# A transformer step in Strassen blocks: sums of weight blocks moved from GpSimd to VectorE

## The chip, the cores and the metric

The kernel runs on one core of a Trainium2 chip. The core has a matrix engine (TensorE, in the profile PE, with its weight loads as PEld), and VectorE (DVE), ScalarE (ACT), GpSimd (POOL) and SyncE (SP), each with a queue that it works off in order; they wait for one another through semaphores. The metric is the time of the slowest core in device microseconds, the median of several executions.

## The reference

One inference step of a one-layer hybrid encoder over 640 tokens (512 of a prompt, 8 times 16 of samples) at a width of 2048, all in float32:

```python
a = rms_norm(x, g_mix); proj = a @ w_in            # q, k, v, forget logits, u
attn = fox_attend(...)                             # 8 heads of 128
ssm = s5_mixer(u, ...)                             # 64 groups, complex diagonal state, GLU
merged = concat(rms_norm(attn), rms_norm(ssm))
h = x + merged @ w_out                             # 2048 x 2048
f = rms_norm(h, g_ffn)
h = h + (silu(f @ w_gate) * (f @ w_up)) @ w_down   # 2048 x 5632, twice, and back
gate = sigmoid(rms_norm(h, g_ple) @ w_ple_gate)    # 2048 x 2048
h = h + gate * (p_i @ w_ple_proj)
```

It returns h with keys, values, log forget values and states.

## The kernel before, in words

Up to about 770 us of the span the kernel computes the input projections, the attention and the state-space part; the change touches little there. Behind that come five matrix products, all made in the same way: the output projection (name o, 8 products), gate and up (g and u, 22 each, in turn), down (d, 28 cells) and the gate of the layer's input embedding (p, 8, called the last projection here).

Each of these products is a 2x2 block product by Strassen's scheme in Winograd's form: seven block products in place of eight. One product works over weight blocks, called units in the code: 328 in all, each 128x1024 float32 (four quarters of 256 columns), four per product in o, g, u and p, and two to four per cell in down. From the four quarters come four sums (`ws`), so that seven stationary operands exist. To keep float32 accuracy each operand is cut in two: a rounded copy (`wh`, ScalarE, line 86) and the remainder (`wl`, VectorE, line 87), in two pieces, first the three raw quarters (768 columns), then the four sums (1024 columns). A unit takes 42 matmuls of 320 columns: seven products, two halves of the rows, and three pairs of high and low parts (lines 1205 to 1207). The staged block `wst` has two buffers, `wh` and `wl` two each, and the sums `ws` one. Of the four sums of a unit GpSimd makes three (lines 109 to 111) and VectorE one (line 112).

The moving side, the activations, is cut in the same way: four quarters (128x320 each) and three sums, made by `winograd_rows` (four operations, lines 118 to 121; one of them overwrites a quarter), then a rounded copy and a remainder (`cut`, lines 1050 and 1051). Results that a later stage reads as activations are summed on GpSimd and stored in DRAM (`keep`); a later `fetch` loads and cuts them. The tiles are called `km` for o (built by `build`), `kf` for gate and up, `kt` for down, `kh` for the last projection.

After the seven block products of a cell the banks of PSUM are evicted (lines 1231 to 1240): two copies on ScalarE, six additions on VectorE, and one addition on GpSimd (line 1240). The first copy, line 1232, marks each eviction in the trace. Then o adds x, d adds the stored h (`accum_op` in a DMA from GpSimd's queue for cells that are not the last of their row, line 1346), and p multiplies and adds the stored h on GpSimd (line 1373).

The program is written in this order, and a planner with modelled costs lays out each engine's queue: in the trace, sums of the next unit stand between the additions of an eviction.

Of the kernel before, what the change touches and what calls it, by code (L numbers as in the profile page):

```python
# [9 lines left out]
F32 = mybir.dt.float32  # L10
# [4 lines left out]
OP = mybir.AluOpType  # L15
# [89 lines left out]

def winograd_weights(nc, q, s):

    tt = nc.gpsimd.tensor_tensor
    tt(s[:, 0], q[:, 0], q[:, 3], op=OP.add)  # L109
    tt(s[:, 1], s[:, 0], q[:, 1], op=OP.subtract)  # L110
    tt(s[:, 3], q[:, 2], s[:, 1], op=OP.subtract)  # L111
    nc.vector.tensor_tensor(s[:, 2], q[:, 1], q[:, 0], op=OP.subtract)


def winograd_rows(eng, q, s):

    tt = eng.tensor_tensor
    tt(s[:, 0], q[:, 0], q[:, 1], op=OP.subtract)  # L118
    tt(q[:, 0], q[:, 2], q[:, 0], op=OP.subtract)
    tt(s[:, 1], q[:, 2], s[:, 0], op=OP.subtract)  # L120
    tt(s[:, 2], s[:, 1], q[:, 3], op=OP.subtract)  # L121
# [43 lines left out]
def hybrid_step(ctx: ExitStack, tc: tile.TileContext, io):  # L165
    nc = tc.nc
# [32 lines left out]
    tc_dr = dp.tile([FT // 2, P, 7, NH2], F32, name="tc_dr")  # L199
    fc_dr = dp.tile([KT // 2, P, 7, NH2], F32, name="fc_dr")  # L200
    hc_dr = dp.tile([KT // 2, P, 7, NH2], F32, name="hc_dr")
# [819 lines left out]
    for k in range(8):  # L1021
        t = gp_.tile([P, NTOK], F32, tag="xg", name=f"gld{k}", bufs=3)
# [4 lines left out]
    for k in range(2):  # L1027
        t = gp_.tile([P, NTOK], F32, tag="xg", name=f"p{k}", bufs=3)
# [17 lines left out]
    def rows(dram, j):  # L1046
        return dram[2 * j * P : 2 * (j + 1) * P, :].rearrange("(a p) n -> p a n", p=P)

    def cut(k, part, x, eng=nc.vector):
        nc.scalar.activation(k[:, 0, part], x, AF.Copy)  # L1050
        eng.tensor_tensor(k[:, 1, part], x, k[:, 0, part].bitcast(F32), op=OP.subtract)  # L1051

    def blocks4(x):
        return x.rearrange("p a (h n) -> p (a h) n", h=2)

    def build(k, b, s, src, i, by):

        nc.sync.dma_start(b, rows(src, i))
        nc.vector.tensor_tensor(b, b, by[:, None, :].to_broadcast([P, 2, NTOK]), op=OP.mult)
        q = blocks4(b)  # L1060
        cut(k, slice(1, 4), q[:, 1:])
        winograd_rows(nc.gpsimd, q, s)
        cut(k, slice(0, 1), q[:, 0:1])
        cut(k, slice(4, 7), s)
        return k
# [6 lines left out]
    def build_early(i):  # L1072
        b = gp_.tile([P, 4, 512], F32, tag="kc", name=f"mb{i}", bufs=2)
        s = gp_.tile([P, 2, 8, P], F32, tag="vc", name=f"ms{i}", bufs=1)
        b = b.rearrange("p a n -> p (a n)")[:, : 2 * NTOK].rearrange("p (a n) -> p a n", a=2)
        s = s.rearrange("p a b n -> p (a b n)")[:, : 3 * NH2].rearrange("p (a n) -> p a n", a=3)
        mk.append(build(kp_view(act_tile(f"km{i}")), b, s, m_dr, i, ssqa if i < 4 else ssqs))
# [65 lines left out]
    def pair(name):  # L1143
        return fo.tile([P, 2, NTOK], F32, tag="R", name=name, bufs=2)
# [12 lines left out]
    def kp_tile(name, i):  # L1157
        if i < 5:
            return kp_view(act_tile(name))
        if i == 5:  # L1160
            return fo.tile([P, 2, 7, NH2], F32R, tag="kp", name=name, bufs=1)
        return xp.tile([P, 2, 7, NH2], F32R, tag="kp", name=name, bufs=KB)

    def seven(name):
        return xp.tile([P, 7, NH2], F32, tag="c7", name=name, bufs=1)

    def keep(eng, c, dram, i):

        winograd_rows(eng, c[:, :4], c[:, 4:])
        nc.sync.dma_start(dram[i], c)  # L1170

    def whole(k, x, eng=nc.vector):
        cut(k, slice(0, 4), x[:, :4])
        cut(k, slice(4, 7), x[:, 4:], eng)
        return k

    later = {}

    def fetch(name, slot, dram, i, eng=nc.vector, late=False):
        k = kp_tile("k" + name, slot)  # L1180
        x = k[:, 1].bitcast(F32)
        nc.sync.dma_start(x, dram[i])
        if late:
            later.setdefault(i // 2 - 2, []).append(lambda: whole(k, x, eng))
            return k
        return whole(k, x, eng)

    def cut_late(u):
        for f in later.pop(u, ()):
# [36 lines left out]
    def strassen(name, kps, after=None, into=None):  # L1226
        ps = products(name, kps, after)
        r = pair("r" + name) if into is None else into
        r11, r12, r21, r22 = blocks(r)
        q = fo.tile([P, NH2], F32, tag="q", name="q" + name, bufs=1)  # L1230
        tt = nc.vector.tensor_tensor
        nc.scalar.activation(q, ps[1], AF.Copy)
        tt(r11, q, ps[2], op=OP.add)
        nc.scalar.activation(r12, ps[3], AF.Copy)
        tt(q, q, ps[6], op=OP.add)
        tt(r22, q, ps[7], op=OP.add)
        tt(r12, r12, ps[5], op=OP.add)
        tt(r21, r22, ps[4], op=OP.subtract)
        tt(r22, r22, ps[5], op=OP.add)
        nc.gpsimd.tensor_tensor(r12, r12, q, op=OP.add)  # L1240
        return r
# [6 lines left out]
    def squares(s, x, t, first, other=nc.vector):  # L1248
        nc.scalar.activation(t, x, AF.Square)
        if first:  # L1250
            nc.vector.tensor_tensor(s, t[:, 0], t[:, 1], op=OP.add)
        else:
            nc.vector.tensor_tensor(s, s, t[:, 0], op=OP.add)
            other.tensor_tensor(s, s, t[:, 1], op=OP.add)
# [4 lines left out]
    for i in range(5, 8):  # L1259
        s = seven(f"sm{i}")  # L1260
# [3 lines left out]
    def scaled(c, x, gain, j):  # L1264

        for a in range(2):
            nc.scalar.activation(c[:, 2 * a : 2 * a + 2], halves(x[:, a]), AF.Copy, scale=gain[:, 2 * j + a : 2 * j + a + 1])

    fk = []
    for j in range(8):  # L1270
        after = None
        if j == 7:
            def after(u):
                for i in (2 * u, 2 * u + 1):
                    if i < 7:
                        fk.append(fetch(f"f{i}", i, fc_dr, i, nc.gpsimd if i == 3 else nc.vector, i == 6))
        r = strassen(f"o{j}", mk, after)
        x = pair(f"x{j}")
        nc.sync.dma_start(x, io["xT"][2 * j : 2 * j + 2].rearrange("a p n -> p a n"))
        nc.vector.tensor_tensor(r, r, x, op=OP.add)  # L1280
        c = seven(f"c{j}")
        scaled(c, r, gffn, j)
        if j < 7:
            keep(nc.gpsimd, c, fc_dr, j)
        else:
            winograd_rows(nc.gpsimd, c[:, :4], c[:, 4:])
            kf7 = kp_tile("kf7", 7)
            fk.append(kf7)
            later.setdefault(1, []).append(lambda: whole(kf7, c))
        nc.sync.dma_start(rows(h_dr, j), r)  # L1290
        squares(ssqh, r, x, j == 0)

    tk, slots = {}, (0, 1, 2, 3, 4, 5, 6, 7)

    def next_t():

        u = len(tk) // 2
        if u < FT // 4:
            for i in (2 * u, 2 * u + 1):
                tk[i] = fetch(f"t{i}", slots[i % 8], tc_dr, i, nc.gpsimd if i == 3 else nc.vector)  # L1300

    for f in range(FT // 2):
        z = strassen(f"g{f}", fk, cut_late if f == 0 else None)
# [9 lines left out]
        c = seven(f"t{f}")  # L1313
        t = c[:, :4].rearrange("p (a h) n -> p a (h n)", a=2)
# [13 lines left out]
    def next_h():  # L1328
        i = ready.pop(0)
        hk[i] = fetch(f"h{i}", hslot[i], hc_dr, i)  # L1330

    for n, (j, us, first, last) in enumerate(cells):
        def after(i, us=us, n=n):
            uses[us[i]] -= 1
            if not uses[us[i]] and n < len(cells) - 4:
                next_t()
            if n < 2 and i:
                next_t()
            if n == len(cells) - 1:
                for _ in range(min(2, 3 - i)):  # L1340
                    if ready:
                        next_h()

        r = strassen(f"d{n}", [tk[i] for u in us for i in (2 * u, 2 * u + 1)], after)
        if not last:
            nc.gpsimd.dma_start(rows(h_dr, j), r, accum_op=OP.add)
            continue
        x = pair(f"hx{j}")
        nc.sync.dma_start(x, rows(h_dr, j))
        nc.vector.tensor_tensor(r, r, x, op=OP.add)  # L1350
        c = seven(f"hc{j}")
        scaled(c, r, gple, j)
        if j in (3, 4, 5):
            winograd_rows(nc.gpsimd, c[:, :4], c[:, 4:])
            hk[j] = whole(kp_tile(f"kh{j}", hslot[j]), c)
        else:
            keep(nc.gpsimd, c, hc_dr, j)
            ready.append(j)
        nc.sync.dma_start(rows(h2_dr, j), r)
        squares(ssqp, r, x, j == 4)  # L1360
    hk = [hk[i] for i in (4, 5, 6, 7, 0, 1, 2, 3)]
    for j in range(7):
# [5 lines left out]
        x = pair(f"pj{j}")  # L1368
        nc.sync.dma_start(x, rows(pj_dr, j))
        nc.vector.tensor_tensor(z, z, x, op=OP.mult)  # L1370
        x = pair(f"hy{j}")
# [5 lines left out]
    x = pair("pj7")  # L1377
# [6 lines left out]
    q = fo.tile([P, NH2], F32, tag="q", name="qp7", bufs=1)  # L1384
    tt = nc.vector.tensor_tensor
# [141 lines left out]
```

## Time and profile before

| | |
|---|---|
| median of 3 runs | 3037.12 us (3029.13 to 3037.15) |
| the profiled execution | 3029.73 us, its span 3027.9 us |
| TensorE, weight loads | 2850.7 us (94%), 2719.3 us (90%) |
| VectorE | 2042.4 us (67%), 2830 instructions |
| GpSimd | 1540.3 us (51%), 1545 instructions |
| ScalarE | 1237.7 us (41%), 1627 instructions |
| mean granted clock of TensorE | 0.983 of full speed |

The span is that of the instructions on the core; the time of the execution is a little longer. Busy time is the union of an engine's instructions. Durations of neighbouring instructions of one engine overlap by some hundredths of a microsecond, and a duration holds what the instruction waits for once it has begun.

### The profile page before, as it was taken

To read this page: it belongs to the slowest core of one execution; us is meant where nothing else is said; L and a number is where in the kernel's file an instruction comes from. 1 tells how busy PE (TensorE), PEld (TensorE's weight loads), DVE (VectorE), ACT (ScalarE), POOL (GpSimd) and SP (SyncE) were. 2 spreads that over 40 slices of the span, in tenths; PEclk is the share of its full clock that TensorE was granted. 3 is DMA by queue.
4 is the path that set the end of the run, shared out by engine and by line. 5 is a ranking of instruction groups with operands and counts; after the bars stand their busy time and mean duration, and the time that the engine had idled before them with its cause. 6 is when DMAs were issued, how large, how long until landed. Compare 5 with 4: busy or idle time off the path is not lost.

```text
span 3027.9 us, 48370 instructions
## 1 busy us (share of the span) xinstructions
PE 2850.7 (94%) x19051; PEld 2719.3 (90%) x19051; DVE 2042.4 (67%) x2830; ACT 1237.7 (41%) x1627; POOL 1540.3 (51%) x1545
## 2 busy tenths in 40 slices
PE   7899999999789889999999999999989999988898
PEld 6789988888788889999999999999989999987887
DVE  8939254455777786666666666666775667788766
ACT  4333365456633443333333333333434344444432
POOL 5612300000666665656565656565564554666665
PEclk9999999999899999999999999999999999999999
DMA  5565744456444623232323232323555455646443
GB/s 165 155 172 168 227 173 154 173 200 209 169 150 159 244 85 117 98 118 98 117 99 115 99 115 99 114 99 114 213 127 164 110 171 164 168 155 243 135 146 129
DMA packets 137494, 449.24 MB, mean 148 GB/s; under 512 B 14097, under 2 KB 34673, under 8 KB 124465
## 3 DMA queue, kind: packets, MB, share of 16 engines
q1 hardware_dynamic: 120032, 396.47, 38.6%
q0 software_dynamic: 15936, 45.47, 6.0%
q10 hardware_dynamic: 1296, 4.20, 0.4%
q8 instruction: 149, 2.44, 0.3%
q14 instruction: 81, 0.66, 0.1%
HBM read 342.25 MB, written 101.18 MB: 146 GB/s over the span
## 4 chain that ended last, share of the span: by engine, by line
POOL 23%; DVE 15%; PE 12%; issue 8%; ACT 6%; DMA 1%; DVEq 0%; POOLq 0%; SPq 0%; ACTq 0%
POOL ws L110 7%; DVE wl L87 7%; POOL ws L109 6%; ACT wh L86 5%; POOL ws L111 5%; PE d L1207 4%; PE d L1205 4%; PE d L1206 4%; POOL t L121 1%; POOL t L118 1%; DVE t L1257 1%; DVE rg L1257 1%; POOL rp L1373 1%; DVE kt L1051 1%; POOL t L120 1%
## 5 line engine op out<-in xcount | busy, mean ns | idle before, releaser
L86 ACT ACTIVATE wh<-ws 128x1024 fp32r<-128x1024 f32 x328 | 347.2, 1058 | 976.4 <-POOL ws L111 957.9
L87 DVE TENSOR_TENSOR wl<-ws,wh 128x1024 fp32r<-128x1024 f32 x328 | 415.9, 1268 | 488.2 <-ACT wh L86 488.0
L109 POOL TENSOR_TENSOR ws<-wst 128x256 f32<-128x256 f32 x328 | 335.4, 1023 | 758.1 <-DVE wl L87 758.1
L87 DVE TENSOR_TENSOR wl<-wst,wh 128x768 fp32r<-128x768 f32 x328 | 413.7, 1262 | 94.3 <-ACT wh L86 94.2
L1205 PE MATMUL d<-kt,wh 128*128 128x320 f32 x1232 | 384.9, 315 | 27.2 <-ACT wh L86 15.2
L1207 PE MATMUL g<-kf,wl 128*128 128x320 f32 x1232 | 380.6, 313 | 15.8 <-DVE wl L87 15.6
L1205 PE MATMUL g<-kf,wh 128*128 128x320 f32 x1232 | 382.1, 311 | 3.5 <-ACT wh L86 3.5
L1205 PE MATMUL u<-kf,wh 128*128 128x320 f32 x1232 | 380.7, 309 | 3.4 <-ACT wh L86 3.3
L1206 PE MATMUL d<-kt,wh 128*128 128x320 f32 x1232 | 381.9, 312 | 0.0
L1206 PE MATMUL g<-kf,wh 128*128 128x320 f32 x1232 | 381.4, 310 | 0.0
L1206 PE MATMUL u<-kf,wh 128*128 128x320 f32 x1232 | 380.3, 309 | 0.0
L1207 PE MATMUL u<-kf,wl 128*128 128x320 f32 x1232 | 379.4, 311 | 0.3 <-DVE wl L87 0.3
L1207 PE MATMUL d<-kt,wl 128*128 128x320 f32 x1232 | 362.6, 314 | 13.1 <-DVE wl L87 13.0
L110 POOL TENSOR_TENSOR ws<-ws,wst 128x256 f32<-128x256 f32 x328 | 357.3, 1089 | 23.1
L86 ACT ACTIVATE wh<-wst 128x768 fp32r<-128x768 f32 x328 | 275.0, 839 | 224.0 <-PE d L1206 74.2
L111 POOL TENSOR_TENSOR ws<-wst,ws 128x256 f32<-128x256 f32 x328 | 289.8, 884 | 21.2
L1205 PEld LDWEIGHTS d<-kt,wh 128*128 128x128 f32 x1232 | 234.8, 191 | 34.1 <-ACT wh L86 20.2
L1207 PEld LDWEIGHTS g<-kf,wl 128*128 128x128 f32 x1232 | 231.5, 189 | 22.9 <-DVE wl L87 22.2
L1207 PEld LDWEIGHTS d<-kt,wl 128*128 128x128 f32 x1232 | 228.6, 191 | 19.0 <-DVE wl L87 18.4
L1205 PEld LDWEIGHTS g<-kf,wh 128*128 128x128 f32 x1232 | 232.5, 189 | 5.3 <-ACT wh L86 5.2
L1205 PEld LDWEIGHTS u<-kf,wh 128*128 128x128 f32 x1232 | 231.3, 188 | 4.2 <-ACT wh L86 4.2
L1206 PEld LDWEIGHTS d<-kt,wh 128*128 128x128 f32 x1232 | 234.9, 191 | 0.0
(501 smaller groups left out, 6489.9 us busy)
## 6 DMA issues: line engine op xcount, KB each, us to landing
wst<-in_w_gate SPq DMA_DIRECT2D x88, 512.0 KB
wst<-in_w_up SPq DMA_DIRECT2D x88, 512.0 KB
wst<-in_w_down SPq DMA_DIRECT2D x88, 512.0 KB
tc_dr<-t SPq DMA_DIRECT2D x22, 1120.0 KB
kt<-tc_dr SPq DMA_DIRECT2D x22, 1120.0 KB
wst<-in_w_qk SPq DMA_DIRECT2D x32, 512.0 KB
kc<-in_cache_k SPq DMA_DIRECT2D x16, 1024.0 KB
vc<-in_cache_v SPq DMA_DIRECT2D x16, 1024.0 KB
```

The costliest lines, as they stand in the source:

```text
L86: a = nc.scalar.activation(wh[:, part], x, AF.Copy)
L87: b = nc.vector.tensor_tensor(wl[:, part], x, wh[:, part].bitcast(F32), op=OP.subtract)
L109: tt(s[:, 0], q[:, 0], q[:, 3], op=OP.add)
L110: tt(s[:, 1], s[:, 0], q[:, 1], op=OP.subtract)
L111: tt(s[:, 3], q[:, 2], s[:, 1], op=OP.subtract)
L118: tt(s[:, 0], q[:, 0], q[:, 1], op=OP.subtract)
L120: tt(s[:, 1], q[:, 2], s[:, 0], op=OP.subtract)
L121: tt(s[:, 2], s[:, 1], q[:, 3], op=OP.subtract)
L1205: nc.tensor.matmul(ps[i], wh[:, a, w], k[:, 0, b], start=f, stop=False)
L1206: nc.tensor.matmul(ps[i], wh[:, a, w], k[:, 1, b], start=False, stop=False)
L1207: nc.tensor.matmul(ps[i], wl[:, a, w], k[:, 0, b], start=False, stop=l)
L1257: nc.vector.tensor_tensor(x, x, s[:, None, :].to_broadcast([P, 2, NTOK]), op=OP.mult)
```

## The change

Three of the four sums of a weight block, which GpSimd made, are made by VectorE, so that it makes all four; their order is a little different (the two that do not depend on each other come first). The sums of activation blocks go from GpSimd to VectorE in the build of the first activations, in the output projection and in the last cells of down; those of gate and up (`keep(nc.gpsimd, c, tc_dr, f)`, line 1318) stay on GpSimd. Two remainders (the sums of the fourth fetched tile, `i == 3`, of gate and up and of down) that GpSimd made go to VectorE, and with them the parameter that chose the engine. GpSimd keeps the addition of line 1240, that of line 1373 and its DMAs.

```diff
--- before.py
+++ after.py
@@ -105,11 +105,11 @@
 
 def winograd_weights(nc, q, s):
 
-    tt = nc.gpsimd.tensor_tensor
+    tt = nc.vector.tensor_tensor
     tt(s[:, 0], q[:, 0], q[:, 3], op=OP.add)
+    tt(s[:, 2], q[:, 1], q[:, 0], op=OP.subtract)
     tt(s[:, 1], s[:, 0], q[:, 1], op=OP.subtract)
     tt(s[:, 3], q[:, 2], s[:, 1], op=OP.subtract)
-    nc.vector.tensor_tensor(s[:, 2], q[:, 1], q[:, 0], op=OP.subtract)
 
 
 def winograd_rows(eng, q, s):
@@ -1046,9 +1046,9 @@
     def rows(dram, j):
         return dram[2 * j * P : 2 * (j + 1) * P, :].rearrange("(a p) n -> p a n", p=P)
 
-    def cut(k, part, x, eng=nc.vector):
+    def cut(k, part, x):
         nc.scalar.activation(k[:, 0, part], x, AF.Copy)
-        eng.tensor_tensor(k[:, 1, part], x, k[:, 0, part].bitcast(F32), op=OP.subtract)
+        nc.vector.tensor_tensor(k[:, 1, part], x, k[:, 0, part].bitcast(F32), op=OP.subtract)
 
     def blocks4(x):
         return x.rearrange("p a (h n) -> p (a h) n", h=2)
@@ -1059,7 +1059,7 @@
         nc.vector.tensor_tensor(b, b, by[:, None, :].to_broadcast([P, 2, NTOK]), op=OP.mult)
         q = blocks4(b)
         cut(k, slice(1, 4), q[:, 1:])
-        winograd_rows(nc.gpsimd, q, s)
+        winograd_rows(nc.vector, q, s)
         cut(k, slice(0, 1), q[:, 0:1])
         cut(k, slice(4, 7), s)
         return k
@@ -1169,21 +1169,21 @@
         winograd_rows(eng, c[:, :4], c[:, 4:])
         nc.sync.dma_start(dram[i], c)
 
-    def whole(k, x, eng=nc.vector):
+    def whole(k, x):
         cut(k, slice(0, 4), x[:, :4])
-        cut(k, slice(4, 7), x[:, 4:], eng)
+        cut(k, slice(4, 7), x[:, 4:])
         return k
 
     later = {}
 
-    def fetch(name, slot, dram, i, eng=nc.vector, late=False):
+    def fetch(name, slot, dram, i, late=False):
         k = kp_tile("k" + name, slot)
         x = k[:, 1].bitcast(F32)
         nc.sync.dma_start(x, dram[i])
         if late:
-            later.setdefault(i // 2 - 2, []).append(lambda: whole(k, x, eng))
+            later.setdefault(i // 2 - 2, []).append(lambda: whole(k, x))
             return k
-        return whole(k, x, eng)
+        return whole(k, x)
 
     def cut_late(u):
         for f in later.pop(u, ()):
@@ -1273,7 +1273,7 @@
             def after(u):
                 for i in (2 * u, 2 * u + 1):
                     if i < 7:
-                        fk.append(fetch(f"f{i}", i, fc_dr, i, nc.gpsimd if i == 3 else nc.vector, i == 6))
+                        fk.append(fetch(f"f{i}", i, fc_dr, i, late=i == 6))
         r = strassen(f"o{j}", mk, after)
         x = pair(f"x{j}")
         nc.sync.dma_start(x, io["xT"][2 * j : 2 * j + 2].rearrange("a p n -> p a n"))
@@ -1281,9 +1281,9 @@
         c = seven(f"c{j}")
         scaled(c, r, gffn, j)
         if j < 7:
-            keep(nc.gpsimd, c, fc_dr, j)
+            keep(nc.vector, c, fc_dr, j)
         else:
-            winograd_rows(nc.gpsimd, c[:, :4], c[:, 4:])
+            winograd_rows(nc.vector, c[:, :4], c[:, 4:])
             kf7 = kp_tile("kf7", 7)
             fk.append(kf7)
             later.setdefault(1, []).append(lambda: whole(kf7, c))
@@ -1297,7 +1297,7 @@
         u = len(tk) // 2
         if u < FT // 4:
             for i in (2 * u, 2 * u + 1):
-                tk[i] = fetch(f"t{i}", slots[i % 8], tc_dr, i, nc.gpsimd if i == 3 else nc.vector)
+                tk[i] = fetch(f"t{i}", slots[i % 8], tc_dr, i)
 
     for f in range(FT // 2):
         z = strassen(f"g{f}", fk, cut_late if f == 0 else None)
@@ -1351,10 +1351,10 @@
         c = seven(f"hc{j}")
         scaled(c, r, gple, j)
         if j in (3, 4, 5):
-            winograd_rows(nc.gpsimd, c[:, :4], c[:, 4:])
+            winograd_rows(nc.vector, c[:, :4], c[:, 4:])
             hk[j] = whole(kp_tile(f"kh{j}", hslot[j]), c)
         else:
-            keep(nc.gpsimd, c, hc_dr, j)
+            keep(nc.vector, c, hc_dr, j)
             ready.append(j)
         nc.sync.dma_start(rows(h2_dr, j), r)
         squares(ssqp, r, x, j == 4)
```

## Rows read from the trace of the kernel before

**Rows 1.** The page, engine totals: busy us (share of span) xinstructions.
```profile
PE 2850.7 (94%) x19051; PEld 2719.3 (90%) x19051; DVE 2042.4 (67%) x2830; ACT 1237.7 (41%) x1627; POOL 1540.3 (51%) x1545
```

**Rows 2.** Timeline of ScalarE, down projection: start us, us, instruction.
```profile
2267.97 0.42 ACT L1232 ACTIVATE qd<-d 128x320 f32<-128x320 f32 x1
...
2292.61 0.42 ACT L1232 ACTIVATE qd<-d 128x320 f32<-128x320 f32 x1
```

**Rows 3.** Stretches cut at eviction copies: busy us (xinstructions) of each engine.
```profile
core 0: us, PE busy (x) PEld busy (x) DVE busy (x) ACT busy (x) POOL busy (x), PEclk, DMA share, GB/s
...
782.00:849.49 67.49, 48.26 (x275) 45.17 (x274) 62.73 (x48) 37.83 (x53) 55.33 (x41) 0.86 0.49 166
...
849.49:1044.49 195.00, 177.97 (x1151) 171.78 (x1151) 138.02 (x148) 77.28 (x96) 126.22 (x119) 0.98 0.50 174
...
1044.49:1089.67 45.18, 35.06 (x197) 32.55 (x196) 43.62 (x38) 25.08 (x29) 27.48 (x20) 0.88 0.54 213
...
1116.90:2153.66 1036.76, 1024.41 (x6920) 1014.54 (x6919) 703.71 (x803) 355.80 (x433) 620.02 (x620) 1.00 0.32 108
...
2246.51:2601.65 355.14, 346.29 (x2328) 343.89 (x2327) 229.78 (x287) 138.30 (x169) 184.86 (x198) 0.99 0.53 150
...
2601.65:2777.67 176.02, 158.10 (x1026) 150.18 (x1024) 139.77 (x149) 78.11 (x95) 118.14 (x108) 1.00 0.54 178
...
2814.16:2987.44 173.28, 160.78 (x1036) 153.25 (x1035) 114.34 (x125) 62.39 (x75) 106.47 (x87) 0.99 0.45 146
```

**Rows 4.** Waits of gate and up: us in total, times, longest us.
```profile
ACT wh L86 <- POOL ws L111: 574.1, 164, 5.2
...
DVE wl L87 <- ACT wh L86: 320.5, 143, 2.6
```

**Rows 5.** Timeline of GpSimd, one weight block of an up projection.
```profile
1563.89 0.98 POOL L109 TENSOR_TENSOR ws<-wst 128x256 f32<-128x256 f32 x1 [2.43 <-DVE wl L87]
...
1566.37 0.74 POOL L111 TENSOR_TENSOR ws<-wst,ws 128x256 f32<-128x256 f32 x1
...
1569.53 0.98 POOL L109 TENSOR_TENSOR ws<-wst 128x256 f32<-128x256 f32 x1 [2.43 <-DVE wl L87]
```

**Rows 6.** Timeline of ScalarE, the same block.
```profile
1567.13 1.06 ACT L86 ACTIVATE wh<-ws 128x1024 fp32r<-128x1024 f32 x1 [3.78 <-POOL ws L111]
```

**Rows 7.** Timeline of VectorE, evictions and blocks of the same stretch.
```profile
1552.35 0.47 DVE L1235 TENSOR_TENSOR qg<-qg,g 128x320 f32<-128x320 f32 x1
...
1552.93 0.49 DVE L1236 TENSOR_TENSOR rg<-qg,g 128x320 f32<-128x320 f32 x1
...
1554.65 0.95 DVE L87 TENSOR_TENSOR wl<-wst,wh 128x768 fp32r<-128x768 f32 x1
...
1568.23 1.23 DVE L87 TENSOR_TENSOR wl<-ws,wh 128x1024 fp32r<-128x1024 f32 x1 [2.54 <-ACT wh L86]
...
1569.49 0.42 DVE L112 TENSOR_TENSOR ws<-wst 128x256 f32<-128x256 f32 x1
```

**Rows 8.** Timeline of GpSimd, one eviction of the last projection.
```profile
2896.79 3.68 POOL L1373 TENSOR_TENSOR rp<-rp,hy 128x1280 f32<-128x1280 f32 x1
```

**Rows 9.** Groups of GpSimd: busy us, mean ns, idle us before, releaser.
```profile
L109 POOL TENSOR_TENSOR ws<-wst 128x256 f32<-128x256 f32 x328 | 335.4, 1023 | 758.1 <-DVE wl L87 758.1
...
L110 POOL TENSOR_TENSOR ws<-ws,wst 128x256 f32<-128x256 f32 x328 | 357.3, 1089 | 23.1
...
L111 POOL TENSOR_TENSOR ws<-wst,ws 128x256 f32<-128x256 f32 x328 | 289.8, 884 | 21.2
```

**Rows 10.** Groups of VectorE, the whole span.
```profile
L87 DVE TENSOR_TENSOR wl<-ws,wh 128x1024 fp32r<-128x1024 f32 x328 | 415.9, 1268 | 488.2 <-ACT wh L86 488.0
...
L87 DVE TENSOR_TENSOR wl<-wst,wh 128x768 fp32r<-128x768 f32 x328 | 413.7, 1262 | 94.3 <-ACT wh L86 94.2
...
L112 DVE TENSOR_TENSOR ws<-wst 128x256 f32<-128x256 f32 x328 | 221.6, 676 | 8.0 <-DMA wst<-in_w_out 1.8
```

**Rows 11.** Timeline of GpSimd, the joint of up and down.
```profile
2184.60 3.50 POOL L1051 TENSOR_TENSOR kt<-kt 128x960 fp32r<-128x960 f32 x1
```

**Rows 12.** Timeline of VectorE, the joint of up and down.
```profile
2185.94 2.44 DVE L112 TENSOR_TENSOR ws<-wst 128x256 f32<-128x256 f32 x1
```

## The prediction

> **What bounds the kernel now.** I read the page's engine totals first [rows 1]: TensorE is busy for 94% of the span, so whatever another engine is relieved of can pay only where TensorE waits. To find those places I took TensorE's own speed from two successive evictions in the down projection [rows 2]: 24.64 us apart with four weight blocks between them, so 6.16 us per block (42 matmuls) when nothing holds it. The stretches come next, cut at the first eviction copy of a product [rows 3]. At 6.16 us a block, the output projection (28 blocks, o1 to o7) would take 172.5 us and takes 195.0; gate and up (41 evictions of 4 blocks, 164) would take 1010 and take 1036.8; the middle cells of down (56 blocks) 345 and take 355.1; its last eight cells (24 blocks) 147.8 and take 176.0; the last projection (24 blocks) 147.8 and takes 173.3. That is 22.5 + 26.6 + 10 + 28.2 + 25.5 = 113 us lost. In gate and up TensorE idles for only 12.4 us of its 26.6.
>
> What is late there, the waits of gate and up say [rows 4]: ScalarE waits 574 us for GpSimd's third sum (line 111), VectorE 320 us for ScalarE. A stretch without evictions shows the ring [rows 5 to 7]: GpSimd's three sums run from 1563.89 to 1567.11, ScalarE copies 1.06 us, VectorE takes the remainder for 1.23 us, and only then (one buffer for the sums) may GpSimd begin the next block, at 1569.53. The ring takes 5.64 us against 6.16 on TensorE: half a microsecond in hand, and whatever else is put on GpSimd eats it. In the last projection it is line 1373, 3.68 us between two sums of a block [rows 8].
>
> **The change part by part.** *Three sums of each weight block go from GpSimd to VectorE (328 blocks).* GpSimd loses 335.4 + 357.3 + 289.8 = 982 us [rows 9]. On VectorE the sum already there takes 0.42 us when GpSimd is quiet, and a dependent operation starts 0.11 us after its forerunner ends [rows 7]. Four sums, two of them dependent on the one before: 4 x 0.42 = 1.7 us in place of the 3.2 us in the ring. The ring becomes 1.7 + 1.06 + 1.23 = 4.0 us, with the first remainder (0.95 us) partly under ScalarE's copy: 2.1 us in hand instead of 0.5.
>
> The price is VectorE's load. Now a block costs it 1.268 + 1.262 + 0.676 = 3.21 us in the mean [rows 10]. Undisturbed the parts are 1.23, 0.95 and 0.42 [rows 7], the rest being waits for a port: VectorE's 0.42 us sum lasted 2.44 us beside a GpSimd operation of 3.50 us, and ended just behind it [rows 11, 12]. With GpSimd's sums gone a block costs 1.23 + 0.95 + 1.68 = 3.86 us, so +0.65. The whole: 328 x 0.65 = 213 us.
>
> *Activation blocks (eight early ones, eight of the output projection, eight of the last norm): four sums of 128x320 each.* VectorE's 320-element operation takes 0.47 us [rows 7], so 1.9 us a set and 46 us for the 24. *Two remainders of 960 columns:* 0.95 us for 768 [rows 7] makes 1.2 each by columns, 2.4 us. VectorE should end near 2042 + 213 + 46 + 2 = 2303 us (76%), GpSimd near 1540 - 982 - 128 = 430 (the 128 are 96 sums at its mean of 1.0 us for 256 columns [rows 9], times 320/256, and the two cuts at four times that mean). No DMA is moved; SyncE's loads of weight blocks are released by readers of the staged block, as before, and now by two engines instead of three.
>
> The question is what VectorE holds in each stage; here [rows 3] give its present busy time. Gate and up: 703.7 + 164 x 0.65 = 810 of a floor of 1010; the activation sums stay on GpSimd there. Output projection: 138.0 + 28 x 0.65 + 7 x 1.9 = 169.5 of 172.5. Last eight cells of down: 139.8 + 15.6 + 15.2 = 170.6, above TensorE's 147.8: VectorE becomes the bound. Last projection: 114.3 + 15.6 = 129.9 of 147.8; but line 1373 stays on GpSimd, and if VectorE were shut out for all of its 3.68 us [rows 8], six times 22 us, the stage would stand at 152, which leaves 21 to gain.
>
> The rows say, then, that both engines pay when they work side by side [rows 10 to 12], and that the pay stops with GpSimd's part; this is in the 0.65 us. The Trainium skill (Perfetto Trace Analysis, Optimizing Scalar/DVE Operations) says more generally that moving work between these two might not help, since they share a read port. By the rows the sum below is 59 us; by that rule it would be what gate and up give, where neither is full, 15 us.
>
> Gains that I take, each below its ceiling because VectorE issues in order and still waits for ScalarE's copies in places. Output projection: VectorE full at 169.5 plus about 0.45 us of wait per block, 182, so 13 of 22.5. Gate and up: 15 of 26.6, the 12.4 of idle and a little more. Middle cells: 4 of 10. Last eight cells: 6 of 28, to 170. Last projection: 15 of 25.5, to 158. The build before the first output block (782 to 849) and the joint to gate and up (1044 to 1090): VectorE is busy 62.7 of 67.5 and 43.6 of 45.2 us [rows 3]; in the second, six blocks with three sums more (7.6), a set (1.9) and a cut (1.2) add 11 us, while 38 operations that lose 0.2 to 0.3 us of port waits each, the mean excess in [rows 10], give 8 to 11 back; in the first, five blocks (6) and six sets (11) add 17 and 48 operations give 10 to 14. I take 4 won in the first, where GpSimd's chain of sums also keeps ScalarE and the block's last cut waiting, 0 in the second, and 2 for the joint to down. Sum: 13 + 15 + 4 + 6 + 15 + 4 + 0 + 2 = 59.
>
> The profiled execution took 3029.7 us, 1.8 more than its span; 3029.7 - 59 = 2971. The median of the three runs lies 7.4 above that execution; I give half of it, and forecast 2974.
>
> Bounds of the unknown costs: below, VectorE's operations shorten further and all stages reach the higher of both floors: 22.5 + 26.6 + 10 + 5 + 21 + 10 for the joints = 95, so 2935; with the last cells at TensorE's floor as well (23 more), 2912. Above, the joints lose 16 instead of winning 6 and nothing is won where VectorE is above 90%: 2971 + 13 + 6 + 22 = 3012.
>
> **The rivals.** *VectorE is the new bound and gives the gain back.* In the output projection, the last cells and the joints it has no room. Then gate and up alone win, 15 us: 3015 by the profiled run. For it: VectorE at 92 to 98% of the floors. Against it: the same sums free it of waits for the port, seen in every line of [rows 10]. (This is also where the rule of the Perfetto Trace Analysis page of the Trainium skill, above, would end.)
>
> *Slower: VectorE's waits stay.* In gate and up VectorE is busy 4.29 us a block (703.7 over 164) and waits 1.95 (320.5 over 164). With 4.94 busy there is room for 1.38 us of waiting in the present 6.32. If an in-order VectorE still waits 1.6 us a block for ScalarE's copies, with the evictions behind it, gate and up take 0.22 x 164 = 36 us more: 3066. It decides from 1.38 us on. For it: ScalarE's copy can also be late for another cause than the sums, a buffer that TensorE still reads. Against it: most of the present wait is GpSimd's 3.2 us, which VectorE will spend working.
>
> *All waits of TensorE go:* 2912 to 2935, as above; against it speaks VectorE's load in the last cells.
>
> **How the numbers follow.** Forecast (2940 to 3005) 0.58; VectorE the bound (3005 to 3035) 0.18; slower (about 3066) 0.16; all waits gone 0.08. A difference of 0.3%, 9 us, is about what a measurement of this kernel can tell. Of the second case 0.11 is still faster than 3028 and 0.07 within; of the third 0.01 within. So faster 0.77, same 0.08, slower 0.15. The range leaves out 0.07 of the last case below, and above it the 0.12 of the slower case that lies beyond 3046: 2928 to 3046. The forecast's own range is 2940 to 3005.
>
> **What would show it.** Right: VectorE's sums of 256 columns near 0.42 us, its line 87 back to 1.23 and 0.95; ScalarE no longer waiting hundreds of microseconds for the sums; the last projection at 25 to 26.5 us per eviction instead of 28; gate and up near 1020 between the same evictions; VectorE at 75 to 77%, GpSimd near 14%. Wrong: VectorE waiting for ScalarE more than 1.4 us a block, TensorE waiting for line 87 in gate and up, evictions late so that TensorE waits for lines 1232 to 1239, or an order of VectorE's queue in which the sums stand behind long operations.

## The result and the profile after

The changed kernel takes 2954.32 us (median of 4 runs, 2950.93 to 2955.17) against 3036.16 for the kernel before (4 runs): 0.9733 of it, 95% interval 0.9721 to 0.9746, 82 us less. The forecast was 2974 us, 63 less than the 3037.12 it started from; the range held the time. The profiled execution's span fell from 3027.9 to 2951.8 us.

The engine totals of the page of the kernel after, which answer to [rows 1]:

```profile
PE 2827.2 (96%) x19051; PEld 2717.0 (92%) x19051; DVE 2265.6 (77%) x3912; ACT 1240.9 (42%) x1627; POOL 420.7 (14%) x463
```

GpSimd lost 1120 us of work, VectorE gained only 223. The groups of VectorE say why; they answer to [rows 9, 10] (busy us, mean ns, idle us before and what ended it):

```profile
L87 DVE TENSOR_TENSOR wl<-ws,wh 128x1024 fp32r<-128x1024 f32 x328 | 421.0, 1284 | 101.4 <-ACT wh L86 101.0
L87 DVE TENSOR_TENSOR wl<-wst,wh 128x768 fp32r<-128x768 f32 x328 | 337.5, 1029 | 169.3 <-ACT wh L86 169.3
L110 DVE TENSOR_TENSOR ws<-wst 128x256 f32<-128x256 f32 x328 | 156.6, 477 | 0.0
L112 DVE TENSOR_TENSOR ws<-wst,ws 128x256 f32<-128x256 f32 x328 | 152.8, 466 | 7.0
L111 DVE TENSOR_TENSOR ws<-ws,wst 128x256 f32<-128x256 f32 x328 | 151.4, 462 | 0.0
L109 DVE TENSOR_TENSOR ws<-wst 128x256 f32<-128x256 f32 x328 | 140.3, 428 | 5.5 <-DMA wst<-in_w_up 0.3
```

A sum that took GpSimd 0.88 to 1.09 us takes VectorE 0.43 to 0.48, the one that VectorE already had fell from 0.68 to that, and the first remainder from 1.26 to 1.03. The second remainder did not get shorter in the mean (1.27 and 1.28); in [rows 10] it had been the one that stood only 0.04 us above its undisturbed 1.23. Of VectorE's 582 us of waiting for ScalarE before the remainders, 270 are left.

The stretches between the same eviction copies, as in [rows 3]:

```profile
core 0: us, PE busy (x) PEld busy (x) DVE busy (x) ACT busy (x) POOL busy (x), PEclk, DMA share, GB/s
...
846.73:1027.78 181.05, 171.86 (x1152) 169.00 (x1152) 153.33 (x257) 77.97 (x94) 6.13 (x7) 1.00 0.50 183
1027.78:1071.80 44.02, 31.91 (x186) 29.21 (x185) 41.02 (x59) 24.92 (x28) 0.87 (x1) 0.92 0.53 211
1098.15:2108.45 1010.30, 1010.30 (x6891) 1010.30 (x6890) 834.29 (x1294) 357.12 (x432) 131.55 (x125) 1.00 0.33 110
...
2194.66:2552.56 357.90, 351.48 (x2355) 349.69 (x2354) 273.34 (x457) 139.58 (x170) 39.94 (x32) 0.99 0.53 151
2552.56:2710.02 157.46, 150.77 (x993) 145.34 (x991) 144.73 (x242) 75.10 (x93) 10.06 (x9) 1.00 0.58 192
2748.56:2913.77 165.21, 158.21 (x1037) 154.50 (x1036) 140.89 (x202) 63.16 (x74) 24.83 (x12) 0.98 0.45 155
```

In gate and up TensorE is busy for all of the 1010.30 us: 41 evictions at 24.64, the very floor taken from [rows 2]. Two blocks there, VectorE's timeline (start us, us, instruction):

```profile
1529.54 1.22 DVE L87 TENSOR_TENSOR wl<-ws,wh 128x1024 fp32r<-128x1024 f32 x1
1530.80 0.42 DVE L109 TENSOR_TENSOR ws<-wst 128x256 f32<-128x256 f32 x1
1531.14 0.42 DVE L110 TENSOR_TENSOR ws<-wst 128x256 f32<-128x256 f32 x1
1531.48 0.42 DVE L111 TENSOR_TENSOR ws<-ws,wst 128x256 f32<-128x256 f32 x1
1531.93 0.43 DVE L112 TENSOR_TENSOR ws<-wst,ws 128x256 f32<-128x256 f32 x1
1534.76 0.96 DVE L87 TENSOR_TENSOR wl<-wst,wh 128x768 fp32r<-128x768 f32 x1 [2.40 <-ACT wh L86]
1535.70 1.23 DVE L87 TENSOR_TENSOR wl<-ws,wh 128x1024 fp32r<-128x1024 f32 x1
1536.96 0.43 DVE L109 TENSOR_TENSOR ws<-wst 128x256 f32<-128x256 f32 x1
```

The four sums take 1.56 us (1530.80 to 1532.36) in place of GpSimd's 3.2, and are done 2.4 us before the next remainder begins. The sums start every 6.16 us, TensorE's own pace. The waits of gate and up (us in total, times, longest), the answer to [rows 4]:

```profile
ACT wh L86 <- issue: 253.2, 58, 4.6
DVE wl L87 <- ACT wh L86: 155.1, 124, 2.7
ACT wh L86 <- DVE ws L112: 131.2, 48, 4.2
ACT wh L86 <- PE g L1206: 119.9, 61, 3.4
...
ACT wh L86 <- PE u L1206: 95.0, 43, 3.0
```

ScalarE's copies wait 131 us for the sums where they waited 574, and 215 us for TensorE to free their buffer. Another 253 us ("issue") they stand idle without a cause that the profile shows.

Where the 76 us of the two spans lie, from the times of the first eviction copy (line 1232) of each product in the traces of four kernels; the two middle kernels are the first two experiments:

| stretch, us | before | weight sums alone | activation sums alone | after | gain | forecast |
|---|---|---|---|---|---|---|
| up to the first eviction | 849.5 | 850.8 | 852.5 | 846.7 | 2.8 | 4 |
| output projection, 7 evictions | 195.0 | 187.2 | 179.0 | 181.0 | 14.0 | 13 |
| first gate, first up | 72.4 | 67.1 | 63.5 | 70.4 | 2.0 | 0 |
| gate and up, 41 evictions | 1036.8 | 1010.3 | 1037.7 | 1010.3 | 26.5 | 15 |
| joint to down | 92.9 | 87.4 | 91.5 | 86.2 | 6.6 | 2 |
| middle cells of down | 355.1 | 360.4 | 354.6 | 357.9 | -2.8 | 4 |
| last eight cells | 176.0 | 170.8 | 165.0 | 157.5 | 18.6 | 6 |
| last cell to first of last projection | 36.5 | 40.5 | 35.0 | 38.5 | -2.0 | - |
| last projection, 6 evictions | 173.3 | 157.7 | 166.7 | 165.2 | 8.1 | 15 |
| last eviction and what follows | 40.5 | 37.6 | 40.4 | 38.0 | 2.4 | - |

### The profile page after: what moved, and what is told of

It is laid out like the page before. It is cut to its first block, busy times and chain, and to the rows that moved or that the text cites. A ratio compares the mean times of both kernels' runs of the same rounds, so it can differ in the third digit from the quotient of the medians.

```text
span 2951.8 us, 47685 instructions
## 1 busy us (share of the span) xinstructions
PE 2827.2 (96%) x19051; PEld 2717.0 (92%) x19051; DVE 2265.6 (77%) x3912; ACT 1240.9 (42%) x1627; POOL 420.7 (14%) x463
## 5 line engine op out<-in xcount | busy, mean ns | idle before, releaser
L87 DVE TENSOR_TENSOR wl<-wst,wh 128x768 fp32r<-128x768 f32 x328 | 337.5, 1029 | 169.3 <-ACT wh L86 169.3
L1207 PE MATMUL d<-kt,wl 128*128 128x320 f32 x1232 | 344.5, 315 | 7.4 <-DVE wl L87 7.3
L1205 PEld LDWEIGHTS g<-kf,wh 128*128 128x128 f32 x1232 | 232.1, 188 | 6.8 <-ACT wh L86 6.8
L1206 PEld LDWEIGHTS g<-kf,wh 128*128 128x128 f32 x1232 | 232.2, 189 | 0.0
L1205 PEld LDWEIGHTS u<-kf,wh 128*128 128x128 f32 x1232 | 231.2, 188 | 1.0 <-DVE rg L1236 0.7
L1206 PEld LDWEIGHTS u<-kf,wh 128*128 128x128 f32 x1232 | 231.2, 188 | 0.0
L1207 PEld LDWEIGHTS u<-kf,wl 128*128 128x128 f32 x1232 | 230.0, 188 | 0.9 <-DVE wl L87 0.9
```

The source lines that it names most:

```text
L87: b = nc.vector.tensor_tensor(wl[:, part], x, wh[:, part].bitcast(F32), op=OP.subtract)
L1205: nc.tensor.matmul(ps[i], wh[:, a, w], k[:, 0, b], start=f, stop=False)
L1206: nc.tensor.matmul(ps[i], wh[:, a, w], k[:, 1, b], start=False, stop=False)
L1207: nc.tensor.matmul(ps[i], wl[:, a, w], k[:, 0, b], start=False, stop=l)
```

## The experiments

The theory to be tested: the loss was the ring of sums, copy and remainder, with one buffer for the sums and GpSimd as its slow member. The rivals: GpSimd's use of the port that it shares with VectorE; the activation sums; VectorE's load.

**The two halves.** The weight sums alone (all else as before), and the rest alone:

```diff
 def winograd_weights(nc, q, s):
 
-    tt = nc.gpsimd.tensor_tensor
+    tt = nc.vector.tensor_tensor
...
```

The second kernel has all other lines of the change's diff, and leaves this function as it was.

> Of the changed kernel's parts only the three sums of weight blocks go to VectorE; activation sums and the two remainders stay on GpSimd. Theory 1 (the ring of sums, copy and remainder through GpSimd was the loss): nearly all of the gain is here, 2965 us or less, gate and up near 1010 us between the same evictions (24.64 each), output projection and last cells a few us behind the full change. Rival (the gain is that GpSimd no longer holds the port beside VectorE): a part of the gain that goes with GpSimd's busy time taken away, 982 of some 1120 us, so also about 2965; the two part in the next runs. Rival (the activation sums carry the gain outside gate and up): about 3000 us.

Measured: 2970.4 us, 0.9791 (0.9777 to 0.9806), 5 us above the 2965 that was expected at most. Gate and up run at 24.64 us, as expected: their whole gain comes from the weight sums.

> The other half: activation sums and the two remainders on VectorE, three sums of each weight block stay on GpSimd. Theory 1: gate and up keep their 26.55 and 23.75 us pattern (1036 us between the same evictions), because the ring is unchanged; outside them the ring has GpSimd to itself, which gives the output projection and the last cells up to 10 us; 3020 us, within 3010 to 3035. Rival (VectorE's load decides): slower than before, 3045 us.

Measured: 2986.09 us, 0.984 (0.9826 to 0.9855), below the range that was expected. Gate and up are as before (1037.7 us, the same waits), but outside them the activation sums alone win 43 us (27 in the output projection and the last cells, where up to 10 were expected), and the two halves (58 and 42 us of span) add up to more than both together (76). The waits of gate and up in this kernel show the ring untouched:

```profile
ACT wh L86 <- POOL ws L111: 575.9, 164, 6.4
DVE wl L87 <- ACT wh L86: 324.4, 144, 2.6
```

Outside gate and up the two kinds of sums shared GpSimd's queue. In the trace before, three of the four sums of an activation block stand between the three of a weight block, which so took from 919.22 to 925.93 instead of 3.2 us:

```profile
919.22 0.93 POOL L109 TENSOR_TENSOR ws<-wst 128x256 f32<-128x256 f32 x1
920.11 0.88 POOL L119 TENSOR_TENSOR c<-c 128x320 f32<-128x320 f32 x1
...
925.20 0.73 POOL L111 TENSOR_TENSOR ws<-wst,ws 128x256 f32<-128x256 f32 x1
```

Taking away either kind breaks this up. I take this to be why the halves overlap; no run tests it by itself.

**Port or ring.** First the port without the ring: the changed kernel, and GpSimd makes three additions per block for nobody.

```diff
             winograd_weights(nc, q, s)
+            e = self.pool.tile([P, 256], F32, tag="w_e", name=f"we{i}", bufs=1)
+            for j in range(3):
+                nc.gpsimd.tensor_tensor(e, q[:, j], q[:, 3], op=OP.add)
```

> The changed kernel, and beside it GpSimd makes three additions of 128x256 per weight block from the staged block into a tile that nobody reads: the port is used as before the change, but nothing waits for these sums except the reload of the staged block. Theory 1 (ring): gate and up stay at 24.64 us per eviction (VectorE's operations lengthen, but there are 2 us in hand); where VectorE is full (output projection, last cells of down) some of the gain is lost; 2965 to 2985 us. Rival (port): VectorE's operations lengthen as before the change, with 0.65 us more of them per block, and most of the gain is gone: 3010 us or more.

Measured: 3113.31 us, 1.0265 (1.025 to 1.028), 159 us above the changed kernel and 79 above the one before. The expectation failed, and the rival's number (3010 us or more) came true: gate and up did not keep 24.64 us. They lose 35 of the 159 us, the output projection 27, the last projection 25. The stretch of gate and up (columns as above) and four of VectorE's sums there:

```profile
1146.45:2191.80 1045.35, 1022.81 (x6894) 1010.97 (x6893) 991.45 (x1298) 359.39 (x433) 643.32 (x618) 1.00 0.30 107
```

```profile
1603.71 0.85 DVE L112 TENSOR_TENSOR ws<-wst 128x256 f32<-128x256 f32 x1
1604.48 0.96 DVE L113 TENSOR_TENSOR ws<-wst 128x256 f32<-128x256 f32 x1
1605.36 0.96 DVE L114 TENSOR_TENSOR ws<-ws,wst 128x256 f32<-128x256 f32 x1
1606.35 0.85 DVE L115 TENSOR_TENSOR ws<-wst,ws 128x256 f32<-128x256 f32 x1
```

In these four sums, beside a busy GpSimd, each lasts twice its 0.42 us. Over the whole span the means of the four are 0.58 to 0.67 us, against 0.43 to 0.48 in the changed kernel; the lowest and the highest:

```profile
L112 DVE TENSOR_TENSOR ws<-wst 128x256 f32<-128x256 f32 x328 | 189.7, 578 | 4.7
...
L115 DVE TENSOR_TENSOR ws<-wst,ws 128x256 f32<-128x256 f32 x328 | 218.8, 667 | 6.9
```

VectorE, with four such sums per block, is busy for 991 of 1045 us: it has become the bound. The additions also hold back the reload of the staged block, but VectorE stands idle for only 4.7 us in all before the first of its sums, so that is not the cause. So the sums may move only because GpSimd falls quiet with them. The prediction's 0.65 us per block rested on that; this experiment's expectation left it out.

Then the ring without the port: ScalarE copies the sums onto themselves behind each block, so that the next sums start later.

```diff
             self.done = (a.ins, b.ins)
+            nc.scalar.activation(s, s, AF.Copy)
+            nc.scalar.activation(s[:, :2], s[:, :2], AF.Copy)
```

> The changed kernel, and behind each block's remainder ScalarE copies the sums onto themselves (1024 and then 512 columns, about 1.7 us), so that the next block's sums start 1.7 us later: the ring is as long as before the change (4.0 + 1.7 = 5.7 us) while GpSimd stays quiet. Theory 1 (ring): the gain is largely lost, gate and up back at 25 us or more per eviction, 2995 to 3040 us. Rival (port): no loss beyond ScalarE's own delay, 2955 to 2970 us.

Measured: 3246.76 us, 1.0709 (1.0691 to 1.0727), 207 us above the expected range. Gate and up (columns as above) take 1164.6 us with VectorE busy for 853.6, hardly more than the 834 of the changed kernel:

```profile
1117.52:2282.14 1164.62, 1066.46 (x6912) 1019.98 (x6911) 853.64 (x1297) 633.18 (x762) 114.79 (x125) 0.99 0.28 96
```

The ring where nothing else is in it, from VectorE's and ScalarE's timelines:

```profile
1708.38 0.43 DVE L111 TENSOR_TENSOR ws<-wst 128x256 f32<-128x256 f32 x1 [1.79 <-ACT ws L90]
...
1714.08 0.42 DVE L111 TENSOR_TENSOR ws<-wst 128x256 f32<-128x256 f32 x1 [0.92 <-ACT ws L90]
```

```profile
1712.32 1.06 ACT L89 ACTIVATE ws<-ws 128x1024 f32<-128x1024 f32 x1 [0.56 <-DVE wl L87]
1713.41 0.63 ACT L90 ACTIVATE ws<-ws 128x512 f32<-128x512 f32 x1
```

It is 5.70 us long, as that of the kernel before (5.64 in [rows 5]), but costs far more: the sign was right, the size was not. My reading, which no run tests, is that in [rows 7] the evictions ran on VectorE while GpSimd summed, and that here evictions and sums stand in one queue and each adds to the ring. But this also loads ScalarE, so a control: the same load in the same place, with nobody waiting for it.

```diff
             self.done = (a.ins, b.ins)
+            e = self.pool.tile([P, 256], F32, tag="w_e", name=f"we{i}", bufs=1)
+            for j in range(5):
+                nc.scalar.activation(e, wl[:, j].bitcast(F32), AF.Copy)
```

> A control for the run in which ScalarE copied the sums onto themselves: the same load on ScalarE at the same place (five copies of 256 columns, about 1.7 us, behind each block's remainder), but from the remainder into a tile that nobody reads, so that the next block's sums do not wait for them. If the ring was what cost there (3247 us, 293 more than the changed kernel): little is lost here, 2955 to 3000 us, gate and up near 24.64 us per eviction. If it was ScalarE's load and order: most of the 293 us is lost here too, above 3150.

Measured: 2956.02 us, 0.9753 (0.9739 to 0.9768). Gate and up:

```profile
1101.59:2112.10 1010.51, 1010.51 (x6891) 1010.51 (x6891) 838.68 (x1297) 678.70 (x1254) 128.15 (x125) 1.00 0.33 110
```

ScalarE is busier than in the ring kernel (678.7 against 633.2 us), and nothing is lost. The wait of the next sums is what costs in the ring kernel.

**How much GpSimd may keep.** One of the four sums, that which depends on no other, back on GpSimd:

```diff
-    tt(s[:, 2], q[:, 1], q[:, 0], op=OP.subtract)
+    nc.gpsimd.tensor_tensor(s[:, 2], q[:, 1], q[:, 0], op=OP.subtract)
```

> The changed kernel with one of the four sums of a weight block, the one that depends on no other, back on GpSimd. Ring: it runs beside VectorE's three, VectorE has a quarter of a sum's time less per block, and nothing is lost: 2945 to 2965 us. Port: three additions per block cost 159 us where they did not feed the ring, so one costs about a third, 50 us: 3005; gate and up, with 2 us in hand, keep 24.64 us either way.

Measured: 2943.27 us, 0.9714 (0.9698 to 0.9731): no loss from the port, rather a gain. The cost of three additions does not divide by three: with one, VectorE is busy for 845 of 1011 us in gate and up, and not full as with three. Beside the changed kernel on one chip:

> The changed kernel with the one independent sum of a weight block on GpSimd, beside the changed kernel on the same chip. If the 7 us in the output projection and 4 in the joint to gate and up are the order's doing and hold: 8 to 12 us below the changed kernel, 0.970. If they were chance between executions: equal.

> The changed kernel once more, beside the next two on the same chip: 0.973 of the time of before, 2950 us against some 3032.

Measured: 2943.82 us, 0.9707 (0.9694 to 0.972), and 2951.75 us, 0.9733 (0.972 to 0.9746): 8 us apart, and their executions do not overlap (2943.22 to 2944.78 and 2949.8 to 2953.55). Behind the first eviction the stages repeat within some 2 us from one execution to the other: output projection 173.8 and 173.2 us (181.0 and 180.2 in the changed kernel), first gate and up 66.8 and 66.6 (70.4 and 71.1), last eight cells 162.7 and 162.6 (157.5 and 157.3). VectorE is not lighter (2280.8 us busy, 15 more): the three sums left to it add up to 578 us, where the four had 601, since beside GpSimd's sum two of them last 0.60 and 0.69 us in the mean instead of 0.43 and 0.46. Why the output projection gains is not settled; the planner lays out other queues.

> The independent sum on GpSimd outside down, on VectorE in down, where GpSimd's one lost 5 us in the last eight cells and 3 in the joint. If the stages add up: 5 to 9 us below the kernel with that sum on GpSimd throughout, 2935 us. Rival (the stages outside gate and up change by several us with every new order of the queues, so that nothing adds up): within 5 us of it on either side.

The sum goes to VectorE for the blocks of down and to GpSimd for all others. Measured: 2945.06 us, 0.971 (0.9696 to 0.9723): the rival. The joint to down returned to 86.6 us, but the last eight cells took 164.5, although VectorE makes all the sums there as in the changed kernel with its 157.5. The next experiment changes gate and up alone, and yet its last eight cells take 166.5 us and its last projection 158.7 (157.5 and 165.2 in the changed kernel). So stages outside gate and up change by up to 9 us without a change in their own sums, as the queues are laid out anew.

**VectorE's room.** The activation sums of gate and up, which the change had left on GpSimd, on VectorE too:

```diff
-        keep(nc.gpsimd, c, tc_dr, f)
+        keep(nc.vector, c, tc_dr, f)
```

> The changed kernel with the activation sums of gate and up on VectorE too (22 sets of four, 1.9 us each). VectorE has 834 us of work in the 1010 us of gate and up, and TensorE does not wait there: no change, 2950 to 2960 us, with 40 us more on VectorE less the port waits that GpSimd's 88 additions cause. Rival (VectorE is nearly full there, too): evictions come late and TensorE waits, 2965 to 2985.

Measured: 2953.05 us, 0.9745 (0.9732 to 0.976), no change, as expected. Gate and up:

```profile
1097.86:2107.50 1009.64, 1009.64 (x6886) 1009.64 (x6885) 818.05 (x1377) 362.89 (x431) 36.31 (x41) 1.00 0.33 110
```

With 84 sums more VectorE is busy for 16 us less: beside GpSimd's sums its other operations had lasted longer (the first remainder 1.04 us in the mean of this stretch, now 0.96; the sums of weight blocks 0.43 to 0.51, now 0.42 to 0.48), and that cost more than the 40 us that these sums cost when it makes them itself.

**The addition left in the last projection.**

```diff
-        nc.gpsimd.tensor_tensor(z, z, x, op=OP.add)
+        nc.vector.tensor_tensor(z, z, x, op=OP.add)
```

> The changed kernel with the addition of the stored h in the last projection (line 1373, 128x1280) on VectorE. There VectorE's remainder lasts 3.8 instead of 1.2 us beside GpSimd's 2.97, and TensorE then waits 0.8 us. Port: VectorE pays 1.4 instead of 2.6 us, evictions go from 25.7 towards 24.9 us, five times 0.8: 2949 to 2952 us. Rival (VectorE's load is what holds the last projection): no change or up to 5 us more.

Measured: 2953.25 us, 0.9746 (0.9732 to 0.9761): no change beyond the noise. In the changed kernel GpSimd's addition holds VectorE's remainder, and TensorE waits (timelines of GpSimd, VectorE, TensorE):

```profile
2854.12 2.97 POOL L1373 TENSOR_TENSOR rp<-rp,hy 128x1280 f32<-128x1280 f32 x1 [11.73 <-DMA hy<-h_dr]
```

```profile
2854.37 3.80 DVE L87 TENSOR_TENSOR wl<-ws,wh 128x1024 fp32r<-128x1024 f32 x1 [1.13 <-ACT wh L86]
```

```profile
2858.23 0.41 PE L1207 MATMUL p<-kh,wl 128*128 128x320 f32 x1 [0.77 <-DVE wl L87]
```

On VectorE it lasts 1.49 us, but its operand comes by DMA, and it stands between two sums of a block:

```profile
2848.39 0.42 DVE L111 TENSOR_TENSOR ws<-ws,wst 128x256 f32<-128x256 f32 x1
2849.66 1.49 DVE L1373 TENSOR_TENSOR rp<-rp,hy 128x1280 f32<-128x1280 f32 x1 [0.85 <-DMA hy<-h_dr]
2851.07 0.42 DVE L112 TENSOR_TENSOR ws<-wst,ws 128x256 f32<-128x256 f32 x1
```

```profile
2852.63 0.41 PE L1205 MATMUL p<-kh,wh 128*128 128x320 f32 x1 [1.19 <-ACT wh L86]
```

A wait for the port went and a wait in the queue came: the last sum is 2.3 us late, and so is TensorE, by 1.2.

## Why the prediction was right

*The ring.* Right for gate and up. 3.2 us of sums became 1.56 (forecast 1.7), and gate and up lost all their loss by this part alone (first experiment); the ring kernel with its control shows that a wait in that place costs without GpSimd. The size was short: I took 15 of 26.6 us, little more than the 12.4 in which TensorE was seen idle, and the whole 26.5 went. Most of the other 14 us can be seen in TensorE's timeline before:

```profile
1560.05 0.31 PE L1207 MATMUL u<-kf,wl 128*128 128x320 f32 x1
1560.20 0.31 PE L1205 MATMUL u<-kf,wh 128*128 128x320 f32 x1
```

A matmul lasts 0.31 us and the next starts 0.15 us after it, so a start that is up to 0.16 us late leaves no idle time. In gate and up of the kernel before, 109 starts come more than 0.02 us late, by 22.4 us in all, of which idle time shows 12.3; in the kernel after none does. The last 4 us are some 30 matmuls more that fell between the two evictions.

Ring and port are not clean rivals, however. In [rows 5] GpSimd's third sum takes 0.74 us; at that pace three would take 2.2 us, so about 1.0 of the 3.2 us may itself have been waiting for the port (an estimate from that row). A kernel that breaks the ring and leaves the work where it is, with a second buffer for the sums, was not run. And of the 76 us some 50 lie outside gate and up, where no run separates ring, queue and port.

*VectorE's load.* Forecast 2303 us, measured 2265.6; GpSimd 430 and 420.7. In the stages the forecast of 169.5, 170.6 and 129.9 us stands against 153.3 (output projection), 144.7 (last cells) and 140.9 (last projection), and 810 against 834 in gate and up. The term of the last cells was mis-sized by 26 us, and with it the gain (6 against 18.6). Two causes can be read off: I added durations, but sums that follow each other start every 0.34 us (1530.80, 1531.14, 1531.48 above), and I left out what the other operations would get back; the addition of the stored h (line 1350) fell from 1.76 us in the mean to 1.48, the second square sum (line 1254) from 1.38 to 0.82. In gate and up the load came out higher than forecast, because GpSimd's activation sums, left there, still lengthen VectorE's operations, as the experiment that moves them shows. By the mix experiment, some 7 us of the 18.6 may be the order of the queues.

*The last projection.* 8.1 against 15. Five of the six evictions took 25.3 to 25.9 us, as forecast (25 to 26.5; before, 27.9 to 29.1). The first took 36.9 instead of 32.5; a wait of 3.3 us of TensorE for ScalarE's copy is part of it, and behind that wait a granted clock of 0.53 of full speed from 2755 to 2760 us, nearly all at the lower level of 1.2 GHz (0.91 over the whole eviction). In the rows above, the addition that stayed on GpSimd still costs a wait per eviction, now by the port alone. The weight sums alone gave 157.7 with the same operations there; which order comes out is the planner's.

*Output projection, start, joints.* 13 forecast, 14.0 measured; 4 and 2.8; 2 and 6.6; 0 and 2.0. The 13 were luck: I had VectorE full there at 169.5 us, it is busy for 153.3 of 181.0, and the halves show that the activation sums alone are worth 16 us, the weight sums alone 8. *Middle cells.* 4 forecast, 2.8 lost; the activation sums alone left them as they were (354.6 us), the weight sums alone lost 5. What holds them is open. *The sum.* The stages won 17 us more than the 59 forecast; stages that came out 34 us better stand against others 17 us worse, so that the total is nearer than its terms.

*The rivals.* That VectorE becomes the bound did not happen in gate and up, with GpSimd quiet; the kernel with three idle additions shows that it would have, at 95% of its time. The slower case would have needed 1.38 us of VectorE's waiting per block; measured 155.1 over 164, 0.95.

The Trainium skill (Perfetto Trace Analysis, Optimizing Scalar/DVE Operations) says that moving work between these two engines might not help, as they share a read port. The kernel with the idle additions agrees with it; the 15 us that I had worked out by it do not, for 76 came: GpSimd was emptied (from 620 to 132 us of work in gate and up), and not kept as busy as before.

The Trainium skill (SBUF — State Buffer, Who interferes with whom) says that a VectorE instruction with two inputs in SBUF contends with a GpSimd instruction that reads SBUF, and that the shared ports are an exclusive lock. The rows of the last projection agree: VectorE's 3.80 us began 0.25 us after GpSimd's 2.97, contain the rest of them, and leave 1.08 us, near the 1.22 to 1.23 that this remainder takes alone.

## What to carry to other kernels

Look for the ring: an engine's operations, the copy and the remainder behind them, and the buffer that lets the next round start; compare its length with the period of the bound engine, and remember that each engine's other work joins it. Before moving work from GpSimd to VectorE, cost VectorE at its undisturbed durations only if GpSimd really falls quiet, for then its old operations get shorter too and pay for much of the new ones (here 1120 us left one engine and 223 reached the other). Before moving an operation that waits for a DMA into the queue that feeds the bound engine, look at what stands behind it there: in the last experiment that wait took back what the port gave.

## What was not expected of the hardware

Three additions of 128x256 per block on GpSimd, feeding nobody, cost 159 us when VectorE made four sums beside them. One such sum, taken over from VectorE, which then made three, cost nothing and went with 8 us less. Beside the three additions VectorE's sums of 256 columns last 0.85 to 0.96 us in the rows shown and 0.58 to 0.67 in the mean, instead of 0.42; GpSimd's additions last 1.04 us in the mean.
